# Layer 2's attention scores: four products over 128 rows, or six over 64 rows in two halves of the array

## The chip, the cores and the metric

The kernel runs on one core of one Trainium2 chip. Its engines are TensorE (PE in the profile; its weight loads are listed apart as PEld), VectorE (DVE), ScalarE (ACT), GpSimd (POOL) and SyncE (SP), which here only issues DMAs. The metric is device time of one execution in microseconds, lower is better. The kernel before took 1371.97 us (median of 3 runs, 1371.66 to 1372.84).

## The reference

The program is one inference step of a two-layer decoder. Layer 1 is multi-scale retention, layer 2 sliding-window attention with grouped queries. Both run over a prompt of 1024 tokens and over 8 single decode tokens. Everything is float32. Layer 2 on the prompt, cut to what matters here:

```python
q = rmsnorm(q.reshape(B, L, SWA_KV_HEADS, SWA_GROUP, SWA_HD), q_gain)   # 2 x 8 heads of 64
k = rmsnorm(k.reshape(B, L, SWA_KV_HEADS, SWA_HD), k_gain)              # 2 key heads
...
kk, vv = band(k), band(v)          # each block of 128 queries sees its own and the block before
scores = jnp.einsum('bnqkgd,bnskd->bnkgqs', qb, kk).astype(jnp.float32) * (SWA_HD ** -0.5)
...
scores = scores - alibi_slopes()[:, :, None, None] * dist.astype(jnp.float32)
scores = jnp.where(valid[None, :, None, None], scores, NEG)
p = sink_softmax(scores, sinks).astype(v.dtype)
o = jnp.einsum('bnkgqs,bnskd->bnqkgd', p, vv)
```

One score is a sum over 64 products, half the height of the 128 x 128 array.

## The kernel before

Products that must be near float32 are made of two parts: a high part, which is the value rounded to float32r (the type that TensorE multiplies here), and a low part, which is the rest. A projection then is three products, high by high, low by high and high by low (lines 1090 to 1092), all into one PSUM tile.

Layer 2 handles the 16 query heads as 8 pairs `p`, and the tokens as three groups `ti` of 384, 384 and 256 (+ 8 decode tokens). `pair_proj` is a generator. It projects one group of queries (`q`) or gates (`g`) of a pair, and gives control back after each of 8 steps over the model width, so that attention work can be put between its matmuls. A query tile leaves PSUM in `q_ev`: ScalarE squares it (line 1409) for the norm, and ScalarE and VectorE split it into high and low. The two heads of a pair come out of the projection in partitions 0 to 63 and 64 to 127. `q_ev` builds for each head a tile of 128 partitions, whose one half is the head's high part and whose other half is its low part (`qs[:, 0]` and `qs[:, 1]`). This takes two ScalarE copies of 64 partitions (lines 1410 and 1411) and two VectorE instructions of 64 partitions, which write to the other half's partitions (lines 1412 and 1414).

The keys `kkh` and `kkl` (high and low) hold each key head twice, in both halves of the partitions. A matmul of `qs[:, j]` with `kkh` over 128 rows therefore gives (high + low query) by high key in one go, and one with `kkl` gives the same by low key.

The attention of a pair on one block of 128 tokens is a unit: 8 x 8 = 64 units. Their steps are `att_s` (scores, ALiBi bias, maximum, exponential), `att_r` (normalise), `att_x` (transpose the weights and split them) and `att_o` (product with the values, gate). In `att_s` the scores of both heads go to one tile `psc` of one PSUM bank, from the pool `scp`, which has two banks; so a unit can write one bank while VectorE still reads the other. VectorE reads each head's scores out of the bank (line 1524), scaled by the query's norm and with the bias added. The first block of a pair has 128 keys, all others 256.

TensorE's order is the order of the code. Each round of the main loop makes the scores of a unit four ahead, then some projection steps (`fill`), the transposes of the next unit, more projection steps, and the value product of the present unit:

```python
    for m in range(NU):
        ...
        sc_(m + L)
        ...
        fill(src, W)
        if m + 1 < NU:
            att_x(units[m + 1])
        ...
        fill(src, W)
        until(G, (u.p, u.ti))
        att_o(u)
        ...
        fill(src, W)
```

The order on the other engines in this part is set by a scheduler when the program is built, and so can shift when instructions are added or taken away. The same ScalarE queue also rounds the next weights that SyncE's DMAs bring (`wh`, line 1077), and GpSimd or VectorE takes the rest (`wl`, line 1080).

Of the kernel before, what the change touches and what calls it, by code (L numbers as in the profile page):

```python
# [7 lines left out]
F32 = mybir.dt.float32  # L8
F32R = mybir.dt.float32r
AF = mybir.ActivationFunctionType  # L10
ALU = mybir.AluOpType
# [62 lines left out]
def _trunk(ctx, tc, nc, a):  # L74
# [20 lines left out]
    mm = nc.tensor.matmul  # L95
# [21 lines left out]
    def rsq(out, in_, n):  # L117
        nc.gpsimd.tensor_tensor(out, in_, mhalf[:in_.shape[0], :n], ALU.pow)
# [689 lines left out]
    for n, s in enumerate(slots):  # L808
        while pes and pes[0][0] <= s.t:
            _, fn, args = pes.pop(0)  # L810
# [7 lines left out]
        while ev and ev[0][0] < end:  # L818
            _, _, fn, args = ev.pop(0)
# [24 lines left out]
    def o_view(half):  # L844

        if half:
            return B_hi, B_lo, B_hif
        return [t.rearrange("p a b -> p (a b)").rearrange("p (k t) -> p k t", k=16) for t in (A_hi, A_lo, A_hif)]
# [271 lines left out]
    O_hi, O_lo, _ = o_view(0)  # L1120
# [94 lines left out]
    def io(tag, bufs, dt=F32):  # L1215
        return iop2.tile([128, 384], dt, tag=tag, bufs=bufs, name=tag)
# [14 lines left out]
    gq = c2p.tile([128, 1], F32, name="gq")  # L1231
# [12 lines left out]
    scp = ctx.enter_context(tc.tile_pool(name="scp", bufs=2, space=PSUM))  # L1244
# [3 lines left out]
    atp = ctx.enter_context(tc.tile_pool(name="atp", bufs=1))  # L1248

    kkh = kvp.tile([128, 2, NP], F32R, name="kkh")  # L1250
    kkl = kvp.tile([128, 2, NP], F32R, name="kkl")
# [137 lines left out]
    Q, G, RQ = {}, {}, {}  # L1389
# [3 lines left out]
    def pair_proj(p):  # L1393
        f = p % 2
        if f == 0 and p > 0:
            slots["q"] = wslot(w_in_swa[:, p * 128:p * 128 + 256])
            slots["g"] = wslot(w_in_swa[:, 1280 + p * 128:1280 + p * 128 + 256])
        qsl, gsl = slots["q"], slots["g"]
        g = p // 4
        lo_, hi_ = slice(0, 64), slice(64, 128)  # L1400
        st = {}

        def q_ev(ti, ps):
            t0, t1 = TG[ti]
            n, npr = t1 - t0, min(t1, NP) - t0
            qs = atp.tile([128, 2, 384], F32R, name="qs", bufs=4)
            qf = qs.bitcast(F32)
            sq = io("sq", 2)
            nc.scalar.activation(sq[:, :n], ps[:, :n], AF.Square)
            nc.scalar.activation(qs[lo_, 0, :npr], ps[lo_, :npr], AF.Copy, scale=gq[lo_])  # L1410
            nc.scalar.activation(qs[hi_, 1, :npr], ps[hi_, :npr], AF.Copy, scale=gq[hi_])
            nc.vector.scalar_tensor_tensor(qs[hi_, 0, :npr], ps[lo_, :npr], gq[lo_], qf[lo_, 0, :npr],
                                           ALU.mult, ALU.subtract)
            nc.vector.scalar_tensor_tensor(qs[lo_, 1, :npr], ps[hi_, :npr], gq[hi_], qf[hi_, 1, :npr],
                                           ALU.mult, ALU.subtract)
            if ti == 2:
                gs = slice(64 * g, 64 * g + 64)
                nc.scalar.activation(Qd[gs, 2 * p, :], ps[lo_, 256:264], AF.Copy, scale=gq[lo_])
                nc.scalar.activation(Qd[gs, 2 * p + 1, :], ps[hi_, 256:264], AF.Copy, scale=gq[hi_])
            Q[p, ti] = qs  # L1420
            st[ti] = sq

        def ms_mm(ti):

            t0, t1 = TG[ti]
            nch = (min(t1, NP) - t0) // 128
            sq = st.pop(ti)
            pm = msp.tile([128, 512], F32, tag="ms", name="pm")
            for i in range(nch):
                mm(pm[:, 2 * i:2 * i + 2], sq[:, i * 128:i * 128 + 128], hsel, start=True, stop=True)  # L1430
            if ti == 2:
                mm(pm[0:2, 256:264], hsel, sq[:, 256:264], start=True, stop=True)
            c0 = t0 // 128
            ee = e9[:, c0:c0 + nch].unsqueeze(2).broadcast_to([128, nch, 2])
            rq = atp.tile([128, 3, 2], F32, name="rq", bufs=4)
            rqn = rq[:, :nch, :]
            rqf = rq.rearrange("p c i -> p (c i)")[:, :2 * nch]
            if ti == 2:
                ms = atp.tile([2, ND], F32, name="ms", bufs=1)
                nc.vector.tensor_copy(ms, pm[0:2, 256:264])  # L1440
                nc.sync.dma_start(out=ms16[2 * p:2 * p + 2, :], in_=ms)

            nc.vector.scalar_tensor_tensor(rqn, pm[:, :2 * nch].rearrange("p (c i) -> p c i", i=2), 1.0 / HD, ee,
                                           ALU.mult, ALU.add)
            rsq(rqf, rqf, 2 * nch)
            RQ[p, ti] = rq

        def g_ev(ti, ps):
            t0, t1 = TG[ti]
            n = t1 - t0  # L1450
            gx = io("sq", 2)
            nc.vector.tensor_tensor(gx[:, :n], ps[:, :n], rbc[:, t0:t1], ALU.mult)
            gt = atp.tile([128, 384], F32, name="gt", bufs=3)
            nc.scalar.activation(gt[:, :n], gx[:, :n], AF.Tanh, scale=0.5)
            nc.vector.scalar_tensor_tensor(gt[:, :n], gt[:, :n], 1.0, gx[:, :n], ALU.add, ALU.mult)
            if ti == 2:
                nc.vector.tensor_scalar(gdec2[:, p, :], gt[:, 256:264], 0.5, None, ALU.mult)
            G[p, ti] = gt

        order = ("q0", "q1", "g0", "q2", "g1", "g2") if p == 7 else ("q0", "q1", "q2", "g0", "g1", "g2")  # L1460
        mms = {(1, 3): 0, (2, 3): 1, (4 if p == 7 else 3, 3): 2}
        for step, (kind, ti) in enumerate(order):
            ti = int(ti)
            isq = kind == "q"
            t0, t1 = TG[ti]
            n = t1 - t0
            while 3 * p + ti - (done["s"] if isq else done["o"]) >= (4 if isq else 3):
                yield 1e9
            ps = pjp.tile([128, 512], F32, tag="pj", name="pj")
            for k in range(8):  # L1470
                proj(ps[:, :n], qsl if isq else gsl, f, t0, t1, first=(k == 0), last=(k == 7), ks=[k])
                if (step, k) in mms:
                    ms_mm(mms[step, k])
                yield 3 * n / 2400.0
                if k == 7:
                    (q_ev if isq else g_ev)(ti, ps[:, :n])
            if p == 7 and kind == "g":
                pend_r.append(ti)
# [6 lines left out]
    for p_ in range(8):  # L1485
        for ti_, (t0_, t1_) in enumerate(TG):
            nch_ = (min(t1_, NP) - t0_) // 128
            for i_ in range(nch_):
                u = Unit()
# [5 lines left out]
    ndp = {}  # L1495

    def bias_tab(h):

        ndp[h] = atp.tile([128, 256], F32, name="ndp", bufs=3)
        nc.gpsimd.tensor_scalar(ndp[h], negd, SLOPE[h], None, ALU.mult)  # L1500

    def att_s(u):
        p, i, c, g = u.p, u.i, u.c, u.g
        if c == 4 and p < 7:
            bias_tab(2 * p + 2)
        if c == 0:
            bias_tab(2 * p + 1)
        qs, rq = Q[p, u.ti], RQ[p, u.ti]
        u0 = 0 if c > 0 else 128
        s0_, s1_ = (c - 1) * 128 + u0, c * 128 + 128  # L1510
        psc = scp.tile([128, 2, 256], F32, tag="sc", name="sc")

        st = atp.tile([128, 2, 257], F32, tag="s", name="s", bufs=6)
        mx = atp.tile([128, 2], F32, name="mx", bufs=4)
        sm = atp.tile([128, 2], F32, name="sm", bufs=4)
        h2 = slice(2 * p, 2 * p + 2)
        nc.gpsimd.tensor_copy(st[:, :, 256], snk[:, h2])
        if u0:
            nc.gpsimd.memset(st[:, :, 0:u0], NEG)
        for j in range(2):  # L1520
            mm(psc[:, j, u0:], qs[:, j, i * 128:i * 128 + 128], kkh[:, g, s0_:s1_], start=True, stop=False)
            mm(psc[:, j, u0:], qs[:, j, i * 128:i * 128 + 128], kkl[:, g, s0_:s1_], start=False, stop=True)
        for j in range(2):
            nc.vector.scalar_tensor_tensor(st[:, j, u0:256], psc[:, j, u0:], rq[:, i, j:j + 1], ndp[2 * p + j][:, u0:],
                                           ALU.mult, ALU.add)
        nc.vector.tensor_reduce(mx, st, mybir.AxisListType.X, ALU.max, negate=True)
        for j in range(2):
            nc.scalar.activation(st[:, j, :], st[:, j, :], AF.Exp, bias=mx[:, j:j + 1], accum_out=sm[:, j:j + 1])
        u.st, u.sm = st, sm
        if i == u.nch - 1:  # L1530
            done["s"] += 1
# [214 lines left out]
    def stream():  # L1746
        for p in range(8):
            yield from pair_proj(p)

    ps = stream()  # L1750
# [53 lines left out]
    fill(ps, 2.0)  # L1804
    dec_cache_ev(0, pt)
    att_s(units[0])
    fill(ps, 2.0)
    att_r(units[0])
# [24 lines left out]
    for m in range(NU):  # L1833
        u = units[m]
# [66 lines left out]
```

## Time and profile before

| | |
|---|---|
| time, median of 3 runs | 1371.97 us |
| span of the profiled execution | 1368.6 us, 3.4 us less than that median |
| TensorE busy over the span | 1313.7 us (96%) |
| VectorE, ScalarE, GpSimd busy | 745.5, 669.1, 760.5 us |
| first and last score matmul | 958.1 and 1254.9 us |
| matmuls on lines 1521 and 1522 | 128 each |

The page gives the span, from the first instruction to the last; the profiled execution's own time is not listed apart from it. A matmul's duration in these rows covers its whole way through the array. Matmuls overlap, so the pace is read from start to start. Likewise a weight load overlaps the matmul ahead of it. Tile shapes are written rows * columns: 128*64 is a weight tile of 128 rows and 64 columns. In rows that group several instructions, the second figure is the time from the first one's start to the last one's end.

### The profile page before, as it was taken

To read this page: it belongs to the slowest core of one execution; us is meant where nothing else is said; L and a number is where in the kernel's file an instruction comes from. 1 tells how busy PE (TensorE), PEld (TensorE's weight loads), DVE (VectorE), ACT (ScalarE), POOL (GpSimd) and SP (SyncE) were. 2 spreads that over 40 slices of the span, in tenths; PEclk is the share of its full clock that TensorE was granted. 3 is DMA by queue.
4 is the path that set the end of the run, shared out by engine and by line. 5 is a ranking of instruction groups with operands and counts; after the bars stand their busy time and mean duration, and the time that the engine had idled before them with its cause. 6 is when DMAs were issued, how large, how long until landed. Compare 5 with 4: busy or idle time off the path is not lost.

```text
span 1368.6 us, 25998 instructions
## 1 busy us (share of the span) xinstructions
PE 1313.7 (96%) x9541; PEld 1251.6 (91%) x9541; DVE 745.5 (54%) x1434; ACT 669.1 (49%) x1690; POOL 760.5 (56%) x886
## 2 busy tenths in 40 slices
PE   6999999999999999897979999998999999999998
PEld 6999999999999999686868889997899999998998
DVE  6943665566556553675752112335576777779321
ACT  5532555555556653675741112244576666667311
POOL 6753656655566753697976553544476666544000
PEclk9999999999999999999989999999999999999999
DMA  6314767667667653665645344442111111112532
GB/s 218 103 59 143 220 211 230 176 214 231 199 215 209 219 156 93 188 176 191 172 150 164 123 154 125 135 131 66 47 50 59 44 47 41 40 34 88 170 84 82
DMA packets 192804, 186.66 MB, mean 136 GB/s; under 512 B 12725, under 2 KB 172525, under 8 KB 192661
## 3 DMA queue, kind: packets, MB, share of 16 engines
q1 hardware_dynamic: 155840, 148.87, 35.9%
q10 hardware_dynamic: 36836, 36.14, 8.3%
q8 instruction: 75, 1.23, 0.4%
q14 instruction: 53, 0.43, 0.1%
HBM read 128.59 MB, written 57.41 MB: 136 GB/s over the span
## 4 chain that ended last, share of the span: by engine, by line
PE 84%; DVE 5%; POOL 4%; DMA 3%; issue 2%; ACT 2%; SPq 0%; ACTq 0%; POOLq 0%; DVEq 0%
PE b L340 7%; PE b L342 7%; PE b L341 7%; PE pj L1090 5%; PE pj L1091 5%; PE pj L1092 5%; PE pj L1141 4%; PE pj L1139 4%; PE pj L1140 4%; PE b L334 4%; PE b L333 4%; PE b L335 4%; PE tr L103 3%; PE S L921 1%; PE S L922 1%
## 5 line engine op out<-in xcount | busy, mean ns | idle before, releaser
L340 PE MATMUL b<-xh,woh 128*128 128x258 f32 x784 | 222.4, 284 | 0.0
L342 PE MATMUL b<-xh,wol 128*128 128x258 f32 x784 | 221.9, 283 | 0.0
L341 PE MATMUL b<-xl,woh 128*128 128x258 f32 x784 | 221.6, 283 | 0.0
L1090 PE MATMUL pj<-A_hi,wh 128*128 128x384 f32 (+1 forms) x512 | 173.0, 338 | 0.0
L1091 PE MATMUL pj<-A_lo,wh 128*128 128x384 f32 (+1 forms) x512 | 165.7, 324 | 0.0
L1092 PE MATMUL pj<-A_hi,wl 128*128 128x384 f32 (+1 forms) x512 | 165.5, 323 | 0.0
L340 PEld LDWEIGHTS b<-xh,woh 128*128 128x128 f32 x784 | 148.2, 189 | 1.2
L341 PEld LDWEIGHTS b<-xl,woh 128*128 128x128 f32 x784 | 148.8, 190 | 0.0
L342 PEld LDWEIGHTS b<-xh,wol 128*128 128x128 f32 x784 | 148.2, 189 | 0.0
L1080 POOL TENSOR_TENSOR wl<-wr,wh 128x1024 fp32r<-128x1024 f32 (+1 forms) x60 | 114.8, 1924 | 46.4 <-DVE wh L1079 22.1
L334 PE MATMUL b<-wol,xh 128*128 128x256 f32 x448 | 126.1, 282 | 1.2 <-DVE wol L224 1.2
L333 PE MATMUL b<-woh,xh 128*128 128x256 f32 x448 | 125.9, 281 | 0.0
L335 PE MATMUL b<-woh,xl 128*128 128x256 f32 x448 | 125.8, 281 | 0.0
L1536 POOL TENSOR_TENSOR s<-s,sm 128x512 f32<-128x512 f32 x64 | 67.7, 1057 | 69.2 <-DVE sm L1535 67.5
L282 POOL TENSOR_TENSOR yl<-yd,yh 128x256 fp32r<-128x256 f32 x64 | 56.3, 879 | 82.0 <-PE od L289 40.3
L1090 PEld LDWEIGHTS pj<-A_hi,wh 128*128 128x128 f32 x512 | 98.0, 191 | 0.2
L1091 PEld LDWEIGHTS pj<-A_lo,wh 128*128 128x128 f32 x512 | 98.0, 191 | 0.0
L1092 PEld LDWEIGHTS pj<-A_hi,wl 128*128 128x128 f32 x512 | 97.4, 190 | 0.0
L224 POOL TENSOR_TENSOR wol<-raw,woh 128x512 fp32r<-128x512 f32 x52 | 68.8, 1331 | 47.8 <-ACT woh L219 46.9
L334 PEld LDWEIGHTS b<-wol,xh 128*128 128x128 f32 x448 | 84.4, 188 | 1.4 <-DVE wol L224 1.4
L333 PEld LDWEIGHTS b<-woh,xh 128*128 128x128 f32 x448 | 84.4, 188 | 0.7
L335 PEld LDWEIGHTS b<-woh,xl 128*128 128x128 f32 x448 | 84.4, 188 | 0.0
(368 smaller groups left out, 3847.0 us busy)
## 6 DMA issues: line engine op xcount, KB each, us to landing
raw<-in_w_in_ret_dram ACTq DMA_DIRECT2D x44, 512.0 KB
st<-in_state_ret_dram SPq DMA_DIRECT2D x64, 256.0 KB
out_dram<-st SPq DMA_DIRECT2D x64, 256.0 KB
wr<-in_w_out_ret_dram SPq DMA_DIRECT2D x32, 512.0 KB
wr<-in_w_in_swa_dram SPq DMA_DIRECT2D x18, 512.0 KB
vb<-vscr SPq DMA_DIRECT2D x64, 128.0 KB
evp<-qks SPq DMA_DIRECT2D x32, 256.0 KB
evx<-vsc SPq DMA_DIRECT2D x32, 256.0 KB
```

What stands on the lines that cost most here:

```text
L224: eng.tensor_tensor(lo, src_of(s, name, sub), hi.bitcast(F32), SUB)
L333: mm(dst, xh, wh, start=a and i == 0, stop=False, skip_group_check=True)
L334: mm(dst, xh, wl, start=False, stop=False, skip_group_check=True)
L335: mm(dst, xl, wh, start=False, stop=z, skip_group_check=True)
L340: mm(dst, wh, xh, start=a, stop=False, **sg)
L341: mm(dst, wh, xl, start=False, stop=False, **sg)
L342: mm(dst, wl, xh, start=False, stop=z, **sg)
L1080: lo_eng[0].tensor_tensor(lo[:, js, :], raw[:, i:i + step, :], hi.bitcast(F32)[:, js, :], ALU.subtract)
L1090: mm(ps, hi[:, k, fs], xh[:, k, t0:t1], start=first and k == ks[0], stop=False)
L1091: mm(ps, hi[:, k, fs], xl[:, k, t0:t1], start=False, stop=False)
L1092: mm(ps, lo[:, k, fs], xh[:, k, t0:t1], start=False, stop=last and k == ks[-1])
L1536: nc.gpsimd.tensor_tensor(st[:, :, 0:256], st[:, :, 0:256], sm.unsqueeze(2).broadcast_to([128, 2, 256]), ALU.mult)
```

## The change

In `q_ev` the high parts of both heads go to one tile `qh` of 128 partitions, and the low parts to another, `ql`. That is one ScalarE copy and one VectorE instruction over all 128 partitions. Nothing crosses between the halves of the partitions any more.

In `att_s` each head uses the 64 rows in which its queries lie: head 0 rows 0 to 63, head 1 rows 64 to 127. There are three products for each head, high query by high key, high by low and low by high, six matmuls over 64 rows. The product of the two low parts, which the old form contained, is left out. The matmuls of the two heads alternate. Each head has a PSUM tile of its own, a whole bank, so a unit takes both banks of `scp`.

In the built program, the six matmuls have a tile of 64 rows and 128 columns, at row 0 for head 0 and at row 64 for head 1.

```diff
         def q_ev(ti, ps):
...
-            qs = atp.tile([128, 2, 384], F32R, name="qs", bufs=4)
-            qf = qs.bitcast(F32)
+            qh = atp.tile([128, 384], F32R, name="qh", bufs=4)
+            ql = atp.tile([128, 384], F32R, name="ql", bufs=4)
             sq = io("sq", 2)
             nc.scalar.activation(sq[:, :n], ps[:, :n], AF.Square)
-            nc.scalar.activation(qs[lo_, 0, :npr], ps[lo_, :npr], AF.Copy, scale=gq[lo_])
-            nc.scalar.activation(qs[hi_, 1, :npr], ps[hi_, :npr], AF.Copy, scale=gq[hi_])
-            nc.vector.scalar_tensor_tensor(qs[hi_, 0, :npr], ps[lo_, :npr], gq[lo_], qf[lo_, 0, :npr],
-                                           ALU.mult, ALU.subtract)
-            nc.vector.scalar_tensor_tensor(qs[lo_, 1, :npr], ps[hi_, :npr], gq[hi_], qf[hi_, 1, :npr],
+            nc.scalar.activation(qh[:, :npr], ps[:, :npr], AF.Copy, scale=gq)
+            nc.vector.scalar_tensor_tensor(ql[:, :npr], ps[:, :npr], gq, qh.bitcast(F32)[:, :npr],
                                            ALU.mult, ALU.subtract)
...
-            Q[p, ti] = qs
+            Q[p, ti] = (qh, ql)
...
     def att_s(u):
...
-        qs, rq = Q[p, u.ti], RQ[p, u.ti]
+        (qh, ql), rq = Q[p, u.ti], RQ[p, u.ti]
...
-        psc = scp.tile([128, 2, 256], F32, tag="sc", name="sc")
+        psc = [scp.tile([128, 512], F32, tag="sc", name="sc") for _ in range(2)]
...
+        ts_ = slice(i * 128, i * 128 + 128)
+        for n_, (qx, kx) in enumerate(((qh, kkh), (qh, kkl), (ql, kkh))):
+            for j in range(2):
+                js = slice(64 * j, 64 * j + 64)
+                mm(psc[j][:, u0:256], qx[js, ts_], kx[js, g, s0_:s1_], start=(n_ == 0), stop=(n_ == 2))
         for j in range(2):
-            mm(psc[:, j, u0:], qs[:, j, i * 128:i * 128 + 128], kkh[:, g, s0_:s1_], start=True, stop=False)
-            mm(psc[:, j, u0:], qs[:, j, i * 128:i * 128 + 128], kkl[:, g, s0_:s1_], start=False, stop=True)
-        for j in range(2):
-            nc.vector.scalar_tensor_tensor(st[:, j, u0:256], psc[:, j, u0:], rq[:, i, j:j + 1], ndp[2 * p + j][:, u0:],
+            nc.vector.scalar_tensor_tensor(st[:, j, u0:256], psc[j][:, u0:256], rq[:, i, j:j + 1], ndp[2 * p + j][:, u0:],
                                            ALU.mult, ALU.add)
```

## The prediction

> **What bounds the kernel now.** I read the page first: busy time of each engine, the forty slices, and the chain of waits that ended last.
>
> ```profile
> PE 1313.7 (96%) x9541; PEld 1251.6 (91%) x9541; DVE 745.5 (54%) x1434; ACT 669.1 (49%) x1690; POOL 760.5 (56%) x886
> PE   6999999999999999897979999998999999999998
> PE 84%; DVE 5%; POOL 4%; DMA 3%; issue 2%; ACT 2%; SPq 0%; ACTq 0%; POOLq 0%; DVEq 0%
> ```
>
> TensorE carries 84% of the chain, and only its first slice falls under 7 tenths. The change lies in layer 2's attention, so next I asked for the two stretches in which scores are made, and for TensorE's own waits.
>
> ```profile
> 957.00:1100.00 143.00, 138.04 (x972) 134.92 (x972) 94.08 (x207) 90.88 (x266) 88.08 (x125) 0.98 0.15 49
> 1100.00:1255.00 155.00, 151.80 (x1123) 148.70 (x1123) 118.58 (x259) 106.09 (x312) 89.48 (x132) 1.00 0.16 51
> ...
> PE pm L1430 <- ACT sq L1409: 4.8, 2, 2.5
> ```
>
> The columns of the first two rows are TensorE, its weight loads, VectorE, ScalarE and GpSimd, busy us in stretches of 143 and 155 us, then the granted clock. TensorE is idle for 5.0 and 3.2 us; 4.8 us of that are two waits for the square of a query tile. VectorE and ScalarE have over 36 us to spare in each stretch. So a nanosecond added to or taken from TensorE's stream here moves the end by nearly that much.
>
> The timeline around one unit's scores gives the present price, and the view of line 1521 the count (each unit issues that line twice: 56 units with 256 keys and 8 with 128).
>
> ```profile
> 1103.23 0.33 PE L1092 MATMUL pj<-A_hi,wl 128*128 128x384 f32 x1
> 1103.40 0.28 PE L1521 MATMUL sc<-kkh,qs 128*128 128x256 f32 x1
> 1103.52 0.28 PE L1522 MATMUL sc<-kkl,qs 128*128 128x256 f32 x1
> 1103.64 0.28 PE L1521 MATMUL sc<-kkh,qs 128*128 128x256 f32 x1
> 1103.75 0.28 PE L1522 MATMUL sc<-kkl,qs 128*128 128x256 f32 x1
> 1103.87 0.34 PE L1090 MATMUL pj<-A_hi,wh 128*128 128x384 f32 x1
> ...
> L1521 PE MATMUL sc<-kkh,qs x128: 222/280/582, 958.1 to 1254.8; 128*128 128x256 f32 x112, 128*128 128x128 f32 x16
> ```
>
> The duration of 0.28 us is a pipelined one. What counts is start to start: four matmuls take 1103.87 - 1103.40 = 0.47 us, 0.118 us each.
>
> **The change, part by part.**
>
> *The matmuls themselves.* Four products over 128 rows become six over 64, in three pairs whose halves use different rows and different PSUM banks. No row of this trace shows two row halves at work, so the price is bounded: 3 x 0.118 us if the halves of a pair run beside each other, 6 x 0.118 us if they follow each other. For a 256-key unit that is -0.118 or +0.236 us. A 128-key unit goes at the weight load's pace of 0.11 us (rows below): -0.11 or +0.22. Over all: 56 x -0.118 + 8 x -0.11 = -7.5 us, or +15.0 us. The nearest rows are the pairs above, where loads and streams of neighbours already overlap although they share all rows; since the halves share neither rows nor bank, I take -7.5 and keep +15.0 for the range.
>
> *Going into 64-row operation and out again.* The stream around every unit is made of 128-row instructions, so this happens 64 times each way. The trace has such places with narrower instructions; here, in layer 1, four transposes of 8 rows stand between 128-row products (TensorE first, then the weight loads of the same place).
>
> ```profile
> 233.33 0.28 PE L341 MATMUL b<-xl,woh 128*128 128x258 f32 x1
> 233.45 0.28 PE L342 MATMUL b<-xh,wol 128*128 128x258 f32 x1
> 233.66 0.41 PE L103 MATMUL od<-ident,evc 8*128 8x8 f32 x4
> 234.00 0.39 PE L340 MATMUL b<-xh,woh 128*128 128x258 f32 x1
> 234.23 0.29 PE L341 MATMUL b<-xl,woh 128*128 128x258 f32 x1
> ...
> 233.33 0.19 PEld L342 LDWEIGHTS b<-xh,wol 128*128 128x128 f32 x1
> 233.66 0.32 PEld L103 LDWEIGHTS od<-ident,evc 8*128 8x128 f32 x4
> 234.00 0.19 PEld L340 LDWEIGHTS b<-xh,woh 128*128 128x128 f32 x1
> 234.11 0.19 PEld L341 LDWEIGHTS b<-xl,woh 128*128 128x128 f32 x1
> ```
>
> Normally a load starts together with the matmul before it (233.33 and 233.33) and the next matmul follows 0.12 us later. At the change of rows the load waits: it comes 0.21 us after the last matmul's start, 0.09 us more than the usual pitch, and then nothing hides it. On the way back the load and its matmul stand at 234.00 together, and the next matmul comes 0.23 us later in place of 0.12: 0.11 us of bare load. A second place prices the way out and the bare load without transposes.
>
> ```profile
> 1277.58 0.29 PEld L1643 LDWEIGHTS o<-pm,vdd 8*128 8x128 f32 x2 [0.90 <-ACT ot L1568]
> 1278.00 0.41 PEld L1645 LDWEIGHTS o<-pm,wr 128*128 128x128 f32 x3
> ...
> 1277.59 0.48 PE L1643 MATMUL o<-pm,vdd 8*128 8x128 f32 x2 [0.64 <-ACT ot L1568]
> 1278.00 0.51 PE L1645 MATMUL o<-pm,wr 128*128 128x16 f32 x3
> ```
>
> Three 128-row loads span 0.41 us, of which the last lasts 0.19: a pitch of 0.11. The two 8-row loads span 0.29 us, so their pitch is 0.10 and fewer rows don't make a load shorter. The second 8-row load thus starts near 1277.69, its matmul a load later at about 1277.80, and the 128-row load 0.20 us after that, 0.09 over the pitch. So each way costs 0.09 us of emptying and 0.11 us of bare load: 0.20, or 0.40 us a unit, 64 x 0.40 = 25.6 us. Lower end: the bare load into the half tiles is hidden after all, 0.29 us a unit, 18.6 us. Upper end: both halves' first loads are bare one after the other, 0.51 us, 32.6 us.
>
> Does any switch of tile shape cost this? The trace says no: with 64 columns the load starts with the matmul before it, and the next one keeps its pitch.
>
> ```profile
> 1101.50 0.33 PE L1092 MATMUL pj<-A_hi,wl 128*128 128x384 f32 x1
> 1101.67 0.28 PE L1563 MATMUL o<-pth,vvh 128*64 128x256 f32 x1
> ...
> 1101.51 0.14 PEld L1563 LDWEIGHTS o<-pth,vvh 128*64 128x64 f32 x1
> ```
>
> It is the number of rows that costs, as far as seen with 8. I take it for 64 too, since these rows are the nearest of the kind; the columns' row keeps zero as a rival.
> The Trainium skill, TensorEngine Tiling (Array Packing), Key Properties, says that changing the tiling mode drains TensorE while changing only the tile doesn't. The trace agrees for rows (0.21 us instead of 0.12) and not for columns (0.17, the pitch of a 384-wide stream); by the page the sum would be the same 25.6 us, and with the columns' row it would be nothing.
>
> *The order on TensorE* changes only at the scores. Here are the rows around the eighteenth unit; sc, qs, qh, ql, kkh and kkl are the scores, queries and keys, pj a projection. Before:
>
> ```order
> L1092 MATMUL pj_13162<-A_hi_7708,wl_12903 128x384
> L1521 MATMUL sc_13210<-kkh_11580,qs_12984 128x256
> L1522 MATMUL sc_13210<-kkl_11581,qs_12984 128x256
> L1521 MATMUL sc_13210<-kkh_11580,qs_12984 128x256
> L1522 MATMUL sc_13210<-kkl_11581,qs_12984 128x256
> L1090 MATMUL pj_13162<-A_hi_7708,wh_12902 128x384
> ```
>
> After:
>
> ```order
> L1092 MATMUL pj_13204<-A_hi_7708,wl_12936 128x384
> L1521 MATMUL sc_13252<-kkh_11580,qh_13020 128x256
> L1521 MATMUL sc_13253<-kkh_11580,qh_13020 128x256
> L1521 MATMUL sc_13252<-kkl_11581,qh_13020 128x256
> L1521 MATMUL sc_13253<-kkl_11581,qh_13020 128x256
> L1521 MATMUL sc_13252<-kkh_11580,ql_13021 128x256
> L1521 MATMUL sc_13253<-kkh_11580,ql_13021 128x256
> L1090 MATMUL pj_13204<-A_hi_7708,wh_12935 128x384
> ```
>
> The four full-height products on one bank have become six on two banks (sc_13252 and sc_13253 in turn), with the same neighbours on both sides.
>
> *PSUM.* A unit now takes both score banks, so its first matmul waits until VectorE has read the unit before; projections, transposes and value products queue behind it in TensorE's order. The two tightest places:
>
> ```profile
> 1024.49 0.86 DVE L1524 SCALAR_TENSOR_TENSOR s<-sc,rq,ndp 128x256 f32<-128x256 f32 x2
> 1233.35 0.87 DVE L1524 SCALAR_TENSOR_TENSOR s<-sc,rq,ndp 128x256 f32<-128x256 f32 x2
> ...
> 1025.26 0.28 PE L1521 MATMUL sc<-kkh,qs 128*128 128x256 f32 x1
> 1233.84 0.28 PE L1521 MATMUL sc<-kkh,qs 128*128 128x256 f32 x1
> ```
>
> The reading ends at 1025.35 and 1234.22, 0.09 and 0.38 us after the next unit's start; elsewhere it ends before it. Cost 0.5 us.
>
> *Splitting the queries.* Of 24 query tiles each loses one ScalarE and one VectorE instruction:
>
> ```profile
> L1410 ACT ACTIVATE qs<-pj,gq x24: 456/562/567, 953.0 to 1232.7; 64x384 fp32r<-64x384 f32 x16, 64x256 fp32r<-64x256 f32 x8
> L1411 ACT ACTIVATE qs<-pj,gq x24: 468/575/578, 953.6 to 1233.7; 64x384 fp32r<-64x384 f32 x16, 64x256 fp32r<-64x256 f32 x8
> L1412 DVE SCALAR_TENSOR_TENSOR qs<-pj,gq,qs x24: 477/610/611, 954.2 to 1235.6; 64x384 fp32r<-64x384 f32 x16, 64x256 fp32r<-64x256 f32 x8
> L1409 ACT ACTIVATE sq<-pj x24: 373/491/494, 952.6 to 1232.5; 128x384 f32<-128x384 f32 x16, 128x264 f32<-128x264 f32 x8
> ```
>
> The square over 128 partitions (0.49 us) is no longer than a copy over 64 (0.56), so the merged instructions cost about what one half did: some 14 us less on each engine, all beside TensorE's work. Only at the two waits for the square can it show, by one copy each: 2 x 0.57 = -1.1 us. There the ScalarE order also moves (wh is the rounding of a loaded weight tile, s the exponentials, pth and ot the operands and results of the value product):
>
> ```order
> L1568 ACTIVATE ot<-o 64x128 x2
> L1077 ACTIVATE wh<-wr 128x512 x2
> L1547 ACTIVATE pth<-tr 128x512
> L1528 ACTIVATE s,sm<-s,mx 128x257 x2
> L1568 ACTIVATE ot<-o 64x128 x2
> L1077 ACTIVATE wh<-wr 128x512
> L1409 ACTIVATE sq<-pj 128x384
> ```
>
> After:
>
> ```order
> L1567 ACTIVATE ot<-o 64x128 x2
> L1077 ACTIVATE wh<-wr 128x512 x3
> L1527 ACTIVATE s,sm<-s,mx 128x257 x2
> L1546 ACTIVATE pth<-tr 128x512
> L1567 ACTIVATE ot<-o 64x128 x2
> L1409 ACTIVATE sq<-pj 128x384
> ```
>
> The weight rounding, which waited for its DMA, now stands ahead of an exponential and a value operand too.
>
> ```profile
> 1029.08 0.63 ACT L1077 ACTIVATE wh<-wr 128x512 fp32r<-128x512 f32 x1 [1.43 <-DMA wr<-in_w_in_swa_dram]
> ...
> 1030.14 0.38 PE L1430 MATMUL pm<-C,sq 128*128 128x2 f32 x2 [2.25 <-ACT sq L1409]
> ```
>
> That wait of 2.25 us may vanish or double; I take +0.6 us, with -2.3 and +2.3 as ends. Together with the 0.5 and the -1.1 this is 0.
>
> **Sum.** 25.6 - 7.5 + 0 = +18.1 us: a span of 1386.7 in place of 1368.6. The median of the runs, 1371.97, lies 3.4 us above the span, and with the same 3.4 us the time is 1390.1.
>
> **The rivals.**
> 1. The halves take turns. The load pitch of 0.11 us doesn't shrink with rows, so six loads served one by one make six turns. +25.6 + 15.0 = +40.6: 1412.6 us. Against it: nothing ties the halves together. The Trainium skill, TensorEngine Tiling (Array Packing), Key Properties, has different tiles load and multiply in parallel; no row here shows it, and by it this rival would fall.
> 2. Faster: 64 rows are entered as freely as 64 columns, and the halves run in pairs. -7.5 us: 1364.5. This decides wherever entering and leaving cost a unit under 7.5 / 64 = 0.117 us; the two places with 8 rows, at 0.20 us each way, speak against it.
> 3. Free entry, but halves in turn: +15.0, 1387.0 us.
> 4. Every change of half empties the array. Then six matmuls have five more such steps: 0.71 + 5 x 0.20 + 0.40 - 0.47 = 1.64 us a unit, +105 us: 1477. The trace has no second half; nothing asks for it.
>
> **How the numbers follow.** Forecast 56%, its own range 1381 to 1397 (0.29 or 0.51 us a unit: 1383.1 or 1397.1, and a lucky ScalarE wait). Rival 1 24%, rival 2 11%, rival 3 5%, rival 4 4%. From 1376 to 1416 the range holds the forecast, rivals 1 and 3, and leaves out 15%. No change within 0.2% (2.7 us, about what a measurement can tell) needs an entry price near 0.117 us: 3%. Faster 12%, slower 85%.
>
> **What would show it.** In the new profile: a gap before the first score matmul's weight load and before the first 128-row load behind the scores, about 0.2 us after the matmul before; score starts in pairs a few ns apart, 0.118 us from pair to pair; from the whole matmul ahead of the scores to the one behind them about 0.8 us in place of 0.64 (1103.23 to 1103.87; the one behind then starts with its bare load, 0.11 us before it can work); ScalarE and VectorE some 14 us less busy. Rival 1 shows six starts 0.11 apart; rival 2 loads that start with the matmul before. The forecast is wrong if the emptying belongs to 8 rows only.

## The result

The changed kernel takes 1390.81 us (median of 4 runs, 1389.98 to 1391.75), the kernel before 1371.82 us on the same chip. The ratio is 1.0146, with a 95% interval of 1.0134 to 1.0158: slower by 1.5%. The forecast was 1390.1 us.

The page of the changed kernel: engine totals and chain.

```profile
span 1388.3 us, 26211 instructions
PE 1331.7 (96%) x9669; PEld 1249.1 (90%) x9669; DVE 732.5 (53%) x1410; ACT 655.4 (47%) x1666; POOL 763.5 (55%) x886
...
PE 84%; DVE 5%; POOL 3%; issue 2%; ACT 2%; DMA 2%; SPq 0%; ACTq 0%; POOLq 0%; DVEq 0%
```

TensorE holds the same 84% of the chain and is 18.0 us longer busy (1331.7 against 1313.7). VectorE is 13.0 us and ScalarE 13.7 us less busy, for the instructions that the merged query split saves; nothing of that is seen in the span. The weight loads are 2.5 us less busy although there are 128 more of them, so loads now run beside each other.

The first score matmul starts at 959.6 us (958.1 before), and the span ends at 1388.3 (1368.6). From there to the end it is 428.7 us in place of 410.5: +18.2 us. The other 1.5 us of the spans' difference lie ahead of the first score, where only the splitting of the first queries was changed. Two runs below with the same splitting make their first score at 957.5 and 958.1 us, so the 1.5 us look like scatter between executions.

The timeline of one unit in the changed kernel, TensorE and then its weight loads:

```profile
1111.71 0.33 PE L1092 MATMUL pj<-A_hi,wl 128*128 128x384 f32 x1
1111.98 0.39 PE L1521 MATMUL sc<-kkh,qh 64*128 64x256 f32 x2
1112.20 0.28 PE L1521 MATMUL sc<-kkl,qh 64*128 64x256 f32 x2
1112.32 0.28 PE L1521 MATMUL sc<-kkh,ql 64*128 64x256 f32 x2
1112.53 0.44 PE L1090 MATMUL pj<-A_hi,wh 128*128 128x384 f32 x1
1112.81 0.34 PE L1091 MATMUL pj<-A_lo,wh 128*128 128x384 f32 x1
...
1111.97 0.19 PEld L1521 LDWEIGHTS sc<-kkh,qh 64*128 64x128 f32 x2 [0.24 <-issue]
...
1112.53 0.19 PEld L1090 LDWEIGHTS pj<-A_hi,wh 128*128 128x128 f32 x1
```

Read it from the top. The last whole-height matmul starts at 1111.71. Its successor's load, which before the change starts together with it, starts at 1111.97, 0.26 us later instead of the matmul pitch of 0.17 (0.09 us of emptying). Two loads and two matmuls then start at once: each "x2" is a pair of halves, and 0.39 us for two matmuls that each last 0.38 says that their starts are a few ns apart. The next pair starts 0.22 us later (0.11 of bare load and 0.118 of streaming), the third 0.12 us after that. Then 0.21 us pass until the first whole-height load, and its matmul needs 0.28 us to the next start in place of 0.17, which is the bare load on the way out. From 1111.71 to 1112.81, the start of the second whole-height matmul behind the scores, there are 1.10 us. In the kernel before this matmul is

```profile
1104.06 0.34 PE L1091 MATMUL pj<-A_lo,wh 128*128 128x384 f32 x1
```

and from 1103.23 to it there are 0.83 us. That is +0.27 us for this unit. In both traces 60 units lie clear of waits and of stretches at half clock; measured between the same two matmuls they take 0.263 us more on average, and 64 x 0.263 = 16.8 us.

TensorE's waits from 957 us on, of the changed kernel:

```profile
PE sc L1521 <- DVE s L1523: 3.9, 2, 3.3
PE pm L1427 <- ACT sq L1409: 3.7, 2, 2.4
...
PE o L1562 <- ACT ot L1567: 0.8, 1, 0.8
```

The first row is new: scores that wait for both banks. Both waits are in one unit, the sixty-second. The scores ahead of it were complete at 1260.35 us, but VectorE read them only from 1264.11 on: its order has a step of the decode tokens ahead of the reading, which waited 1.74 us for GpSimd, and then rounded weights (1.40 us). VectorE first, then TensorE:

```profile
1262.29 0.15 DVE L1592 TENSOR_TENSOR r<-r,rbc 16x8 f32<-16x8 f32 x1 [1.74 <-POOL r L118]
...
1262.78 1.40 DVE L1080 TENSOR_TENSOR wl<-wr,wh 128x512 fp32r<-128x512 f32 x1
1264.11 0.47 DVE L1523 SCALAR_TENSOR_TENSOR s<-sc,rq,ndp 128x256 f32<-128x256 f32 x1
...
1265.03 0.47 DVE L1523 SCALAR_TENSOR_TENSOR s<-sc,rq,ndp 128x256 f32<-128x256 f32 x1
...
1264.63 0.38 PE L1521 MATMUL sc<-kkh,qh 64*128 64x256 f32 x1 [3.35 <-DVE s L1523]
1265.55 0.58 PE L1521 MATMUL sc<-kkh,qh 64*128 64x256 f32 x1 [0.54 <-DVE s L1523]
```

### The profile page after: what moved, and what is told of

Read it like the earlier page. It is cut to its first block, busy times and chain, and to the rows that moved or that the text cites. A ratio compares the mean times of both kernels' runs of the same rounds, so it can differ in the third digit from the quotient of the medians.

```text
span 1388.3 us, 26211 instructions
## 1 busy us (share of the span) xinstructions
PE 1331.7 (96%) x9669; PEld 1249.1 (90%) x9669; DVE 732.5 (53%) x1410; ACT 655.4 (47%) x1666; POOL 763.5 (55%) x886
## 4 chain that ended last, share of the span: by engine, by line
PE 84%; DVE 5%; POOL 3%; issue 2%; ACT 2%; DMA 2%; SPq 0%; ACTq 0%; POOLq 0%; DVEq 0%
PE b L340 7%; PE b L342 7%; PE b L341 7%; PE pj L1090 6%; PE pj L1091 5%; PE pj L1092 5%; PE pj L1141 4%; PE pj L1139 4%; PE pj L1140 4%; PE b L334 4%; PE b L333 4%; PE b L335 4%; PE tr L103 4%; PE sc L1521 2%; PE S L921 1%
## 5 line engine op out<-in xcount | busy, mean ns | idle before, releaser
L1090 PE MATMUL pj<-A_hi,wh 128*128 128x384 f32 (+1 forms) x512 | 177.4, 347 | 0.0
```

The source lines that it names most:

```text
L1090: mm(ps, hi[:, k, fs], xh[:, k, t0:t1], start=first and k == ks[0], stop=False)
```

## The experiments

Each experiment is compared with the kernel before, run on the same chip. Its median was 1371.71 us beside the extra matmul of 64 rows, head 1 left out, head by head and the first form of two units; 1370.57 beside the full-height control; 1371.19 beside the last two runs.

Some accounts need the granted clock. In these traces it is full but for stretches of 3.4 us or a multiple, in which it is half (0.50 from 969.2 to 972.5 us in the kernel before). By estimate a microsecond at half clock costs up to half a microsecond. From 957 us on the kernel before and the changed one both spend 10.2 us at half clock.

### One extra matmul of 64 rows, and its control of 128 rows

These measure the disputed price by itself. The edit to the kernel before, with 64 rows and with 128:

```diff
+        mm(psc[:, 0, 128:136], qs[0:64, 0, i * 128:i * 128 + 128], kkh[0:64, g, s0_:s0_ + 8], start=True, stop=True)
         for j in range(2):
             mm(psc[:, j, u0:], qs[:, j, i * 128:i * 128 + 128], kkh[:, g, s0_:s1_], start=True, stop=False)
```

```diff
+        mm(psc[:, 0, 128:136], qs[0:128, 0, i * 128:i * 128 + 128], kkh[0:128, g, s0_:s0_ + 8], start=True, stop=True)
```

> The kernel before, with one extra matmul of 64 rows and 8 columns ahead of each unit's scores; its result is overwritten. This is the price of entering and leaving by itself. Theory: 0.09 us of emptying and 0.11 us of bare load each way, 0.40 us a unit, 64 x 0.40 = 25.6 us over the kernel before: 1397.4 us, 1391 to 1400. Rival (only matmuls of 32 rows and fewer cost this): the pitch of one load, 0.11 us a unit, 7 us: 1379 us.

> The kernel before, with one extra matmul of 128 rows and 8 columns ahead of each unit's scores; its result is overwritten. This is the control for the one of 64 rows: the same instruction count and no change of rows. Theory: one load's pitch of 0.11 us a unit, 64 x 0.11 = 7.0 us over the kernel before, 1378.9 us. Rival (the extra instruction itself or its place disturbs the stream): as slow as with 64 rows, 1391 to 1400 us.

Measured: 1392.40 us with 64 rows, ratio 1.015 (1.0135 to 1.0165), +20.7 us. With 128 rows 1379.76 us, ratio 1.0062 (1.0045 to 1.008), +9.2 us. The same instruction with half the rows costs 11.5 us more. The 64-row timeline (TensorE, loads), then that of the control:

```profile
1112.77 0.33 PE L1092 MATMUL pj<-A_hi,wl 128*128 128x384 f32 x1
1113.03 0.27 PE L1520 MATMUL sc<-kkh,qs 64*128 64x8 f32 x1
...
1113.46 0.28 PE L1523 MATMUL sc<-kkl,qs 128*128 128x256 f32 x1
...
1113.03 0.18 PEld L1520 LDWEIGHTS sc<-kkh,qs 64*128 64x128 f32 x1 [0.24 <-issue]
```

```profile
1106.95 0.33 PE L1092 MATMUL pj<-A_hi,wl 128*128 128x384 f32 x1
1107.12 0.17 PE L1520 MATMUL sc<-kkh,qs 128*128 128x8 f32 x1
...
1107.35 0.28 PE L1523 MATMUL sc<-kkl,qs 128*128 128x256 f32 x1
```

From the last whole-height matmul to the second score product it is 0.69 us with 64 rows and 0.40 with 128. Without the extra matmul these two steps would be 0.17 and 0.12, 0.29 us. So the visit to 64 rows costs 0.40 us in the stream, as forecast, and the full-height matmul 0.11. Over the 61 units clear of waits and half clock the means are 0.395 and 0.114 us. In the time, 25.6 us are expected of the visit and 20.7 were measured (interval 18.5 to 22.6): the stream shows the price in full, and about 5 us are won back elsewhere. TensorE's waits from 957 us on, 7.0 us in place of 9.0, are 2 us of that; the rest stays open. The two runs differ by 11.5 us where the streams differ by 64 x 0.281 = 18.0: the profiled control waits 9.5 us in place of 7.0 and spends 17.1 us at half clock in place of 10.2, which by estimate costs it 2.5 + 3.4 = 5.9 us. The rival that only narrow matmuls of 32 rows and fewer cost this (1379 us) falls.

### Head 1's matmuls left out

```diff
         for n_, (qx, kx) in enumerate(((qh, kkh), (qh, kkl), (ql, kkh))):
-            for j in range(2):
+            for j in range(1):
...
-        psc = [scp.tile([128, 512], F32, tag="sc", name="sc") for _ in range(2)]
+        psc = [scp.tile([128, 512], F32, tag="sc", name="sc")] * 2
```

> The changed kernel without head 1's three score matmuls; head 1's scores are read from head 0's bank, so the computation is changed. A unit then needs one bank and the two banks of the pool alternate again. Theory (the halves work side by side, entering and leaving the 64-row form is the price): nothing saved on TensorE's stream, and the 3.9 us of waits for score banks go: 1387 us, 1384 to 1391; a unit from its first score start to the first whole matmul's start stays at 0.55 us. Rival (the halves share streaming or loading): 3 x 0.11 us a unit less, 21 us, 1366 to 1370.

Measured: 1385.73 us (1382.65 to 1387.60), ratio 1.01 (1.0082 to 1.0117). Taking away half of the score matmuls leaves the unit as long as it was:

```profile
1108.22 0.33 PE L1092 MATMUL pj<-A_hi,wl 128*128 128x384 f32 x1
1108.48 0.38 PE L1521 MATMUL sc<-kkh,qh 64*128 64x256 f32 x1
...
1109.03 0.45 PE L1090 MATMUL pj<-A_hi,wh 128*128 128x384 f32 x1
```

From 1108.22 to 1109.03 there are 0.81 us, with all six matmuls 0.82. The second half is free, loads included. The 5 us that the kernel gains on the changed one are of the size of the bank waits (3.9 us), which are gone from TensorE's list there; with one bank a unit the two banks take turns again. That these waits are the whole gain is not shown: all of TensorE's waits from 957 us on fall only from 11.9 to 10.5 us, and the profile is of the shortest of the four executions (1382.65 us), which from 957 us on has no stretch at half clock. The other three, with the changed kernel's mean clock (0.985 and 0.986), took 1384.94 to 1387.60 us.

### Head by head in program order

```diff
-        for n_, (qx, kx) in enumerate(((qh, kkh), (qh, kkl), (ql, kkh))):
-            for j in range(2):
-                js = slice(64 * j, 64 * j + 64)
+        for j in range(2):
+            js = slice(64 * j, 64 * j + 64)
+            for n_, (qx, kx) in enumerate(((qh, kkh), (qh, kkl), (ql, kkh))):
```

> The changed kernel with its six score matmuls in another order: three of head 0, then three of head 1, in place of alternating heads. Theory (the halves work side by side, but matmuls start in program order): head 1's first can start only with head 0's third, so five steps of 0.118 us in place of two and a bit: +0.236 us for each of 56 units and +0.22 for 8, +15.0 us over the changed kernel's 1390.8, 1405.8 us; starts 0.118 apart but for one pair. Rival (each half runs its own queue, the order doesn't matter): 1390.8, still pairs. Rival (the pairs of starts in the trace hide a shared resource, and the halves take turns anyway): 1390.8 too, but six steps that each last as long as now.

Measured: 1387.22 us (1386.05 to 1387.61), ratio 1.0112 (1.0095 to 1.0129). The expected loss of 15 us did not come. The timeline shows the pairs that the alternating order has, though in the program all of head 0 stands ahead of head 1:

```profile
1109.26 0.33 PE L1092 MATMUL pj<-A_hi,wl 128*128 128x384 f32 x1
1109.52 0.39 PE L1521 MATMUL sc<-kkh,qh 64*128 64x256 f32 x2
1109.74 0.29 PE L1521 MATMUL sc<-kkl,qh 64*128 64x256 f32 x2
1109.86 0.28 PE L1521 MATMUL sc<-kkh,ql 64*128 64x256 f32 x2
1110.08 0.44 PE L1090 MATMUL pj<-A_hi,wh 128*128 128x384 f32 x1
```

Program order would give kkh, kkl, kkh, kkh, kkl, kkh with single starts. Head 1's first product (the fourth matmul) starts with head 0's first, so it overtakes two matmuls that wait. The theory that matmuls start in program order falls; that a half takes its next work as soon as it is free takes its place, within a reach that a run below shows. The order of the code is thus the order in which TensorE is handed its matmuls, not always the one in which it starts them. This kernel is 3.6 us faster than the changed one with the same unit in the stream (0.82 us from 1109.26 to 1110.08). Its waits for banks are shorter, 1.2 us in place of 3.9, since the scheduler ordered VectorE otherwise there; that part was not tried by itself.

### Two units in one stretch

```diff
+        for u, o_, u0, mx in todo:       # two units, columns 0 and 256 of the two banks
...
+            for n_, (qx, kx) in enumerate(((qh, kkh), (qh, kkl), (ql, kkh))):
+                for j in range(2):
+                    js = slice(64 * j, 64 * j + 64)
+                    mm(psc[j][:, o_ + u0:o_ + 256], qx[js, ts_], kx[js, u.g, s0_:s1_], start=(n_ == 0), stop=(n_ == 2))
...
     def sc_(m):
-        if m < NU:
+        if m < NU and m % 2 == 0:
```

> The changed kernel with the scores of two units in one stretch of 12 matmuls, every other round of the main loop (the first four units stay single): 34 stretches of 64 rows in place of 64. The two units share the two banks, 256 columns each. Theory (the price is per entry and exit, about 0.40 us a stretch): 30 x 0.40 = 12 us less, 1379 us, within 3 us for waits on the banks that come or go. Rival (the price belongs to each 64-row matmul): no change, 1391 us.

Measured: 1384.83 us (1384.32 to 1389.84), ratio 1.0103 (1.0083 to 1.0124): 6.0 us less than the changed kernel, half of what was expected. The stream did what the theory says:

```profile
1093.60 0.33 PE L1092 MATMUL pj<-A_hi,wl 128*128 128x384 f32 x1
1093.87 0.39 PE L1525 MATMUL sc<-kkh,qh 64*128 64x256 f32 x2
...
1094.56 0.28 PE L1525 MATMUL sc<-kkh,ql 64*128 64x256 f32 x2
1094.77 0.45 PE L1090 MATMUL pj<-A_hi,wh 128*128 128x384 f32 x1
```

One stretch of six pairs takes 1.17 us (1093.60 to 1094.77). Twice the 0.82 us of a single unit are 1.64. The difference of 0.47 holds one usual pitch of 0.17, which the two stretches count twice; the bare load on the way out, which isn't in either figure, adds 0.11. So about 0.4 us are saved for each of 30 stretches, 12 us. The profile is of the longest of the four executions (1389.84 us), in which nearly all of this came back. The new waits of TensorE from 957 us on, and the row of that whole stretch with its granted clock (0.99 in the changed kernel):

```profile
PE o L1567 <- ACT ot L1572: 7.5, 6, 2.2
PE pm L1427 <- ACT sq L1409: 5.9, 5, 2.2
...
957.00:1388.00 431.00, 410.03 (x2943) 388.81 (x2941) 230.62 (x504) 213.02 (x630) 186.91 (x264) 0.97 0.21 63
```

The two rows of waits were 0.8 and 3.7 us in the changed kernel: 8.9 us of new waits, against 3.9 us of bank waits that are gone. All of TensorE's waits from 957 us on are 17.5 us in place of 11.9, and 23.9 us are at half clock in place of 10.2; by estimate that is 5.6 + 6.8 = 12.4 us, the 12 us that the stream saves. The other three executions took 1384.32 to 1385.16 us. Two units at once hand ScalarE four exponentials close together, and in four of the six places of the first row the output copies stand behind them. In the two longest (2.06 and 2.20 us) they don't: there ScalarE had waited 1.99 us for the DMA of a weight tile, and 4.33 us for VectorE. Whether two units at once bring that about was not tried.

In a version of this with all of head 0's six matmuls ahead of head 1's six, the reach of the overtaking could be seen.

> As the kernel with two units in one stretch, but all six matmuls of head 0 ahead of all six of head 1. Theory after the head-by-head run (each half takes its next matmul as soon as it is free, whatever stands ahead of it in program order for the other half): head 1's first starts within some ns of head 0's first, six matmuls ahead of its turn; six pairs, 1384 to 1387 us like the kernel with alternating heads. Rival (it can overtake only two or three): the second half starts later by 0.118 us for each matmul that it can't overtake, up to 30 x 6 x 0.118 = 21 us more.

Measured: 1386.73 us, ratio 1.0115 (1.0097 to 1.0132).

```profile
1088.44 0.38 PE L1528 MATMUL sc<-kkh,qh 64*128 64x256 f32 x1
1088.66 0.28 PE L1528 MATMUL sc<-kkl,qh 64*128 64x256 f32 x1
1088.78 0.27 PE L1528 MATMUL sc<-kkh,ql 64*128 64x256 f32 x1
1088.79 0.39 PE L1528 MATMUL sc<-kkh,qh 64*128 64x256 f32 x2
1089.01 0.28 PE L1528 MATMUL sc<-kkl,qh 64*128 64x256 f32 x2
...
1089.25 0.28 PE L1528 MATMUL sc<-kkh,qh 64*128 64x256 f32 x1
...
1089.70 0.45 PE L1090 MATMUL pj<-A_hi,wh 128*128 128x384 f32 x1
...
1088.78 0.19 PEld L1528 LDWEIGHTS sc<-kkh,qh 64*128 64x128 f32 x2
```

The full list has three rows of single matmuls, three rows of two, and from 1089.25 on three of single ones again, up to the whole-height matmul. The last line is a pair of loads: the second half's first load starts with the first half's fourth, so it overtakes two loads that wait, as in the run before. Its first matmul is in the row of 1088.79 and starts at 1088.787, with the first half's third (1088.780); the other matmul of that row, the first half's fourth, starts at 1088.895. So three waiting matmuls are overtaken here, and not all five behind the first: neither expectation was right in full, the reach is short. The three steps more cost 3 x 0.118 x 30 = 10.6 us in the stream, and yet the time is only 1.9 us above the alternating order's. The profiled executions, 1386.08 and 1389.84 us, even lie the other way round: from 957 us on TensorE waits 8.0 us there and 17.5 in the alternating order, and 10.2 us are at half clock against 23.9, by estimate 9.5 + 6.8 = 16.3 us less.

### The kernel before with a later sum of squares

The trace of before shows two waits of over 2 us for the squared queries, each followed by a stretch of half clock. Both kernels have them, so their removal is the way to a version faster than either.

```diff
-        mms = {(1, 3): 0, (2, 3): 1, (4 if p == 7 else 3, 3): 2}
+        mms = {(1, 6): 0, (2, 6): 1, (4 if p == 7 else 3, 6): 2}
```

> The kernel before, with the matmuls that sum the squared queries (line 1430) three projection steps later, about 1.5 us, so that TensorE meets the square when ScalarE has made it. Two waits of 2.54 and 2.25 us for that square, and the stretch of half clock of 3.4 us behind each, are what this aims at. Theory: most of both waits goes, and with it the half clock: 2 x (1.5 + 1.7) = 6 us at most, 1366 to 1370 us. Rival (the query norms then come later, and the scores wait for them instead): 1371.7 us or more.

Measured: 1367.75 us (12 runs) against 1371.19, ratio 0.9975 (0.9966 to 0.9984): faster than both kernels, by less than the 6 us at most. The wait for the square falls from 4.8 to 0.8 us, but 2.8 us of others take part of its place (the first row was 0.3 before):

```profile
PE o L1565 <- DVE ptl L1548: 3.1, 2, 2.4
...
PE pm L1430 <- ACT sq L1409: 0.8, 1, 0.8
```

The clock is in the stretches around these places: columns as in the prediction's first windows, the granted clock third from the end. The kernel before in both stretches, then this one in the second:

```profile
962.00:975.00 13.00, 10.46 (x57) 9.62 (x55) 5.25 (x15) 5.84 (x20) 4.63 (x6) 0.87 0.26 81
1028.00:1042.00 14.00, 11.86 (x78) 11.66 (x79) 7.47 (x17) 9.53 (x25) 10.29 (x13) 0.88 0.28 90
```

```profile
1028.00:1042.00 14.00, 11.85 (x87) 11.15 (x87) 8.99 (x23) 10.41 (x31) 11.99 (x16) 1.00 0.30 90
```

In this stretch the busy time is the same, and at the full clock it holds 87 matmuls in place of 78. In the first stretch the clock is 1.00 too. From 957 us on the profiled execution has 3.4 us at half clock in place of 10.2.

## Why the prediction was right

- The price of entry and exit, 0.40 us a unit, is right in each of its parts: 0.09 us of emptying each way (0.26 us to the first load where the pitch is 0.17; 0.21 where it is 0.12) and 0.11 us of bare load each way. The extra matmul of 64 rows has shown it by itself (0.395 us on average), and its control that it isn't the instruction.
- Halves side by side, -7.5 us: right. The run without head 1 is the proof, since its stream is the same. Rival 1 (halves in turn, 1412.6 us) and rival 4 (emptying between halves, 1477) fall with it, and with the row of 64 rows rivals 2 and 3.
- The sum of the two, 18.1 us, stands against 16.8 us in the stream: 1.3 us too much.
- The term for banks was mis-sized: 0.5 us was forecast from the two tightest places of the old trace, 3.9 us were measured, at a place that wasn't among them. There VectorE's order, which the scheduler sets, had a wait of 1.74 us for GpSimd and a rounding of 1.40 us ahead of the reading of scores.
- The wait for the squares fell by 1.1 us (4.8 to 3.7), where the shorter copies and the moved ScalarE order together were put at 0.5. The first of the two waits fell from 2.54 to 1.35 us; the second stayed (2.25 and 2.37), where the two terms nearly cancelled in the forecast too.
- The 0 for all side effects was a lucky sum. TensorE's waits from 957 us on grew by 2.9 us (9.0 to 11.9). With the 16.8 us of the stream that makes 19.7, and 18.2 were measured from the first score on; the 1.5 us between them stay open. The clock doesn't give them. From 962 to 975 us the changed kernel has the full clock (0.87 before), but from 1028 to 1042 us it has 0.76 (0.88 before), and from 957 us on both kernels spend 10.2 us at half clock. The two rows of the changed kernel:

```profile
962.00:975.00 13.00, 11.64 (x77) 10.54 (x77) 5.10 (x15) 5.60 (x20) 5.06 (x7) 1.00 0.26 82
1028.00:1042.00 14.00, 11.63 (x60) 10.12 (x59) 6.34 (x15) 6.96 (x20) 10.59 (x15) 0.76 0.38 123
```

- ScalarE and VectorE won 13.7 and 13.0 us, forecast some 14, and their shares of the chain are what they were (2% and 5%).
- The time came within 0.7 us of the forecast, the span within 1.6 us (1386.7 against 1388.3); 1.5 us of the latter lie ahead of the first score, which the forecast doesn't treat.

## What to carry to other kernels

Matmuls of half height in the two row halves really run side by side, loads too; but each visit from a full-height stream cost 0.40 us here, and a pair saves one step of 0.118 us. Count visits before products: with one product in four saved, a visit would have to hold the work of four units to pay. And where a unit takes all of a pool's banks, look for the longest instruction or wait that a scheduler may put ahead of the reader, not only for the tightest place of the old order.

## What was not expected of the hardware

- Work for the other row half overtakes work that waits. In both runs that could show it a load overtook two loads; its matmul overtook two matmuls in the one and three in the other, and not five.
- A visit to tiles of 64 rows costs a full-height stream 0.40 us, as much as the prediction read off tiles of 8 rows. A tile of 128 rows and 64 columns follows at the usual pitch (0.17 us): of these changes of shape only that of the rows costs.
- After waits of 2.25 and 2.54 us on TensorE the granted clock was halved for a while in the kernel before (0.88 and 0.87 over stretches of 14 and 13 us), so these short waits cost more than themselves; with the later sum of squares the waits are gone and the clock is 1.00 over both stretches. The length of a wait doesn't decide it: the profiled execution without head 1's matmuls waited up to 2.87 us and stayed at the full clock from 957 us on, while after one wait of 1.81 us, in the last run of two units, the clock was halved.

```profile
PE o L1564 <- DVE ptl L1547: 3.5, 2, 2.9
...
957.00:1381.00 424.00, 409.73 (x2754) 381.25 (x2752) 234.16 (x504) 213.02 (x631) 188.23 (x264) 1.00 0.22 65
```
